# RWKV-7 outputs as rows of head and token, a unit's own products in one run, Gram products that alternate between heads, and value rows centred ahead

## The chip, the core and the metric

The kernel runs on one core of one Trainium2 chip. The core has five engines that work side by side: TensorE (PE in the profile; PEld is its weight load), VectorE (DVE), ScalarE (ACT), GpSimd (POOL) and SyncE (SP), whose queue issues nearly all DMAs here. PE writes PSUM alone: 128 partitions with eight banks of 512 float32 each. The metric is the device time of one execution in microseconds (us); the median over several runs is compared.

## The reference

One attention layer and one recurrent layer over 1024 latent and 256 context tokens, 1024 features. The change lies in the recurrent layer's RWKV-7 branch (512 features, 8 heads of 64), which runs over the tokens in both directions, the context first:

```python
def step(s, inp):                      # s: 64x64 per head
    r_t, w_t, k_t, v_t, kk_t, b_t = inp
    sa = jnp.einsum('bhij,bhj->bhi', s, kk_t)
    s = s * w_t[:, :, None, :] - sa[..., None] * b_t[:, :, None, :] + v_t[..., None] * k_t[:, :, None, :]
    y = jnp.einsum('bhij,bhj->bhi', s, r_t) if emit else None
    return s, y
...
yf = y.astype(jnp.float32)             # y: both directions' sum
mean = jnp.mean(yf, axis=-1, keepdims=True)
var = jnp.mean(jnp.square(yf - mean), axis=-1, keepdims=True)
yn = ((yf - mean) * lax.rsqrt(var + RWKV_GN_EPS)).reshape(y.shape[:2] + (BRANCH_W,))
yn = (yn * gn_w + gn_b).astype(v.dtype)
bonus = jnp.sum(r * k_bonus * r_k, axis=-1, keepdims=True) * v
```

Each row i of the state takes in its own value `v_t[i]` alone, so an output's 64 values depend linearly on the 64 values of `v`; `mean` and `var` go over these 64.

## The kernel before

All is float32; a float32 product shows as two records on PE, a transpose as one. Layer 1 first projects its inputs and, per head pair `j` (128 features), stores to DRAM the keys and normalised keys (`KK`, by `rw_keys`), the values as rows of tokens (`VT`, by `rw_values`: ten PE transposes for each of four pairs), the receptance (`US`), decays (`SG`) and rates (`AS`).

The recurrence is worked in chunks of 64 tokens. A **unit** is four chunks (256 tokens, block `q`; `q == 0` is the context and gives no output) of one head pair `j` in one direction `d`: 8 jobs of 5 units, 40 units, 32 of them latent. A unit goes through these functions:

- `rw_front` loads its inputs, makes running sums of the decays (`cs_ps`), takes their exponentials into `E`, `AK`, `AR`, scales them by the keys and the receptance (L1505, L1506), forms `BK`, and multiplies per head and chunk `BK` by `AKR` (the Gram products, `g_ps`, L1533: 64 rows of the array, 128 columns; head 0 rows 0 to 63, head 1 rows 64 to 127). The result is masked into `la` (DVE) and `gm` (ACT copy, POOL mask). Transposes of `BK` give `BT`; `AK` and the products `la` by `V` fill `R` (`rh_ps`).
- `rw_invert` inverts a job's 32x32 blocks in 31 steps of two DVE instructions (L1586, L1588), spread over other work by `PACE`.
- `rw_solve` makes `At` and `UV` from `R` in three products; `rw_trans` makes `PH` (carries the state over a chunk) and `RT` (what the state adds to a chunk's outputs).
- `rw_scan` goes chunk by chunk: `BT` by `UV` and `PH` by the last state `S` add up in `st_ps`; ACT scales that into the next `S` (L1674). Two ACT copies put `S` into a 128x128 block-diagonal tile `sd` (L1681); `RT` by `sd` and, per head, `gm` by `UV` add up in `yo_ps`, with tokens as rows and both heads' features as columns. `Y` takes the sum, then adds the other direction's.
- `rw_bonus` and `rw_readout` close a block once both directions are done: mean (L1721, L1722), centring (L1724), variance, scale, two transposes (`yt_ps`), gate, store.

Block-wise order in `rwkv`: for unit `b`, `upto("s", b + 2)`, `fronts(b + 12)`, `upto("t", b + 1)`, bonus, scan, and from `b >= 28` `Final.after(b)`, the output projection (`fe_ps`). The first ten fronts run ahead, five between projections of layer 1. This order is only what is traced: a planner that simulates the engines puts each engine's instructions in order, bound by data, by buffers and by explicit edges. `tc.keep_in_program_order(ins)` is such an edge: `ins` comes behind the instruction traced just before it on its engine, but others may come in between. `rw_invert` has raised priority.

PSUM banks in this stage: tag `f` two (all five tiles of a front after the tenth: `cs_ps`, two `g_ps`, `bk_ps`, `rh_ps`; later `fe_ps`), `s` one, `p` two, `t`, `y`, `r` one each; `PB` and `FB` are these counts.

Of the kernel before, what the change touches and what calls it, by code (L numbers as in the profile page):

```python
# [29 lines left out]
def constants():  # L30
# [5 lines left out]
    c["k_ones2"] = b  # L36
    p = np.zeros((128, 128), np.float32)
# [37 lines left out]
    gm[0, :, 0], gm[0, :, 1] = tc_ > sr, tc_ >= sr  # L75
    gm[1, :, 0], gm[1, :, 1] = tc_ < sr, tc_ <= sr
# [44 lines left out]
PB = (1, 1, 1, 1, 1)  # L121
# [52 lines left out]
class K:  # L174
# [1064 lines left out]
    def rw_init(self):  # L1239
# [12 lines left out]
        tri = fp.tile([128, 2, 256], F32, name="tri0", tag="kkf", bufs=2)  # L1252
        nc.sync.dma_start(out=tri, in_=a["k_tri"].rearrange("d p k -> p d k"))
        C["tri"] = fp.tile([128, 2, 256], F32R, name="tri", bufs=1)
        nc.vector.tensor_copy(out=C["tri"], in_=tri)
# [34 lines left out]
    def rw_pre(self, sp):  # L1290
        nc, a = self.nc, self.a
        self.ones2 = sp.tile([128, 128], F32, name="ones2k")
        nc.sync.dma_start(out=self.ones2, in_=a["k_ones2"])
        self.e12 = sp.tile([128, 1], F32, name="e12")
        nc.vector.memset(self.e12, 1e-12)
# [74 lines left out]
    def rwkv(self):  # L1370
        nc, tc, a = self.nc, self.tc, self.a
        with ExitStack() as st:
# [13 lines left out]
            C["S"] = [kp.tile([128, 128], F32, name=f"S{i}") for i in range(4)]  # L1386
            self.ns = 0
# [5 lines left out]
            def fronts(n):  # L1393
                while self.nf < min(n, 40):
                    invert(PACE[0])
                    self.rw_next_front()
                    if self.nf == 10:
                        for t in C["S"]:
                            nc.vector.memset(t, 0.0)

            def upto(what, n):
                while done[what] < min(n, 40):
# [20 lines left out]
            for b in range(40):  # L1423
# [8 lines left out]
                if i == 0 and d == 0:  # L1432
                    Y = wp.tile([128, 8, 128], F32, name="Y", bufs=2)
# [28 lines left out]
    def rw_front(self, F, q, wp, bufs):  # L1462
# [5 lines left out]
        tags = [(t, dict(zip("sptyrf", PB + (FB,)))[t]) for t in ("sfff" if self.nfront < 5 else "rfty" if self.nfront < 10 else "ffff")]  # L1468
# [23 lines left out]
        AK, AR = AKR[:, :, 0, :], AKR[:, :, 1, :]  # L1492
        nc.scalar.activation(out=AK, in_=ps[:, :, 128:256], func=AF.Exp, scale=K0)
# [6 lines left out]
        kv, kf = v3(kk[:, 0]), v3(kk[:, 1])  # L1500
# [23 lines left out]
        W = 128 if lat else 64  # L1524
        for h in range(2):
            z = slice(64 * h, 64 * h + 64)
            ps = self.rps([128, 4, 128], "g_ps", *tags[1])
            for ci in range(4):
                i, c = divmod(ci, 2)
                zc = slice(64 * c, 64 * c + 64)  # L1530
                w = BK[z, i, 128 * c:128 * c + 128]
                x = AKR[z, i, :, zc] if lat else AK[z, i, zc]
                nc.tensor.matmul(ps[:, ci, 0:W], w, x, start=True, stop=True)  # L1533
            nc.vector.tensor_tensor(out=la[:, h], in0=ps[:, :, 0:64], in1=mask[:, 0:64].unsqueeze(1).to_broadcast([128, 4, 64]),
                                    op=ALU.mult)
            if lat:
                nc.scalar.copy(out=gm[:, h], in_=ps[:, :, 64:128])
# [619 lines left out]
```

## Time and profile before

| | |
|---|---|
| median of 3 runs | 2480.39 us (2474.9 to 2482.06) |
| profiled execution | 2487.22 us |
| its span | 2485.4 us, 45290 instructions |
| PE, PEld busy | 2275.4 us, 1892.6 us |
| DVE, ACT, POOL busy | 1568.8 us, 1177.3 us, 931.4 us |
| HBM | 145 GB/s over the span |

The span runs from the first to the last profiled instruction; 1.8 us of the profiled execution lie around it. Matmuls are pipelined and a record's end is modelled, so that a record's time holds a tail in which the next one already runs; start-to-start distances say what a record costs its successor. The granted clock is that of PE: 1.0 is 2.4 GHz, 0.5 is 1.2 GHz.

### The profile page before, as it was taken

The page shows a single profiled execution, that of the slowest core. Times are in us where ns is not written, and L with a number is a line of the kernel's source. Part 1 is how long each engine was busy: PE and PEld are TensorE (multiplying, and loading weights), DVE is VectorE, ACT ScalarE, POOL GpSimd, SP SyncE. Part 2 cuts the span into 40 slices and gives each one's busy share as a digit, 9 for nine tenths or more (in the row PEclk, how much of TensorE's full clock was granted, in tenths as well). Part 3 has the DMA queues.
Part 4 walks back from the last instruction along what each step waited for, and adds up shares of the span by engine and source line. Part 5 has one row for each costly group of instructions (what it writes and reads, how often), then busy time and mean ns, then how long its engine had stood idle before and what let it go on. Part 6 is the DMA issues. An engine that isn't in the chain of part 4 may idle for free. (4 is left out here: it accounts for less than half of the span.)

```text
span 2485.4 us, 45290 instructions
## 1 busy us (share of the span) xinstructions
PE 2275.4 (92%) x16647; PEld 1892.6 (76%) x16647; DVE 1568.8 (63%) x3175; ACT 1177.3 (47%) x2695; POOL 931.4 (37%) x959
## 2 busy tenths in 40 slices
PE   4999999999999989779899889999968999998997
PEld 3877888777878877668778778788757877887775
DVE  6255532368667867455486696457797776777425
ACT  5354434456556555532323221366435656665334
POOL 1253235201011654511033244224745464655512
PEclk8999999999999989889999999999858989999999
DMA  8433344682222766843454544574534343444522
GB/s 280 132 123 119 126 147 146 196 254 93 80 68 90 200 199 183 225 165 110 144 164 150 164 158 136 173 257 134 155 85 131 107 122 97 115 134 126 168 73 92
DMA packets 351428, 361.69 MB, mean 146 GB/s; under 512 B 83106, under 2 KB 283055, under 8 KB 350438
## 3 DMA queue, kind: packets, MB, share of 16 engines
q1 hardware_dynamic: 341894, 330.34, 43.5%
q10 hardware_dynamic: 9168, 24.25, 3.2%
q0 software_dynamic: 144, 4.19, 0.4%
q8 instruction: 132, 2.16, 0.4%
q14 instruction: 90, 0.74, 0.1%
HBM read 260.07 MB, written 100.10 MB: 145 GB/s over the span
## 5 line engine op out<-in xcount | busy, mean ns | idle before, releaser
L158 PE MATMUL g_ps<-xl,w_hi 128*128 128x512 f32 x1056 | 268.0, 399 | 1.0 <-ACT w_hi L192 1.0
L158 PEld LDWEIGHTS g_ps<-xl,w_hi 128*128 128x128 f32 x1056 | 198.9, 191 | 44.0 <-issue 1.9
L158 PE MATMUL s_ps<-k,q 128*128 128x256 f32 (+1 forms) x704 | 199.9, 381 | 7.6 <-DVE pn L700 4.3
L441 POOL TENSOR_TENSOR al_acc<-al_acc,al_t 128x512 f32<-128x512 f32 x98 | 129.0, 1316 | 185.6 <-ACT al_t L439 155.5
L196 DVE TENSOR_TENSOR w_lo<-w_raw,w_hi 128x256 fp32r<-128x256 f32 (+1 forms) x184 | 131.2, 769 | 86.6 <-PE g_ps L158 45.3
L187 ACT COPY pt<-pt_ps 128x512 f32<-128x512 f32 (+1 forms) x203 | 102.1, 506 | 139.3 <-PE pt_ps L161 133.7
L1586 DVE TENSOR_TENSOR tmp<-L,X 80x112 f32<-80x112 f32 (+25 forms) x279 | 136.4, 489 | 17.8 <-DMA L<-LD 8.9
L1588 DVE TENSOR_TENSOR X<-X,tmp 80x112 f32<-80x112 f32 (+25 forms) x279 | 140.6, 504 | 6.5
L158 PE MATMUL g_ps<-xl,w_lo 128*128 128x512 f32 x528 | 137.8, 395 | 0.0
L161 PE MATMUL pt_ps<-ident,p 128*128 128x128 f32 x704 | 118.1, 283 | 17.7 <-DVE pt L185 7.5
L158 PE MATMUL g_ps<-xhi,w_hi 128*128 128x512 f32 (+1 forms) x528 | 118.2, 366 | 8.9 <-DVE ac_res L283 4.7
L161 PEld LDWEIGHTS pt_ps<-ident,p 128*128 128x128 f32 x704 | 80.8, 141 | 52.9 <-DVE pt L185 14.8
L158 PEld LDWEIGHTS s_ps<-k,q 128*128 128x128 f32 x704 | 109.9, 200 | 14.6 <-DVE p L700 7.1
L695 ACT ACTIVATE p<-p,mn 128x1280 f32<-128x1280 f32 (+1 forms) x96 | 103.4, 1077 | 35.7 <-DVE p L700 35.5
L439 ACT ACTIVATE al_t<-al_w,condT 128x512 f32<-128x512 f32 x98 | 70.8, 722 | 101.7 <-POOL al_acc L441 60.9
L158 PE MATMUL g_ps<-xhi,w_lo 128*128 128x512 f32 (+1 forms) x528 | 118.2, 362 | 0.0
L881 POOL TENSOR_TENSOR bias<-namask,tt 128x384 f32<-128x384 f32 x64 | 67.5, 1055 | 125.9 <-DVE mn L890 52.0
L158 PEld LDWEIGHTS g_ps<-xl,w_lo 128*128 128x128 f32 x528 | 98.2, 188 | 21.1 <-issue 1.4
L158 PE MATMUL g_ps<-xlo,w_hi 128*128 128x512 f32 (+1 forms) x528 | 112.8, 356 | 0.0
L158 PEld LDWEIGHTS g_ps<-xhi,w_hi 128*128 128x128 f32 x528 | 90.0, 194 | 29.5 <-DVE qraw L549 5.4
L158 PE MATMUL g_ps<-AKR,BK 64*128 64x128 f32 (+1 forms) x640 | 91.1, 335 | 22.6 <-DVE AKR L1505 14.8
L158 PEld LDWEIGHTS g_ps<-xhi,w_lo 128*128 128x128 f32 x528 | 89.0, 189 | 18.9 <-issue 5.8
(438 smaller groups left out, 5869.4 us busy)
## 6 DMA issues: line engine op xcount, KB each, us to landing
w_raw<-rec_w_in SPq DMA_DIRECT2D x33, 512.0 KB
hfw<-FW SPq DMA_DIRECT2D x32, 512.0 KB
w_raw<-attn_w_in SPq DMA_DIRECT2D x13, 1024.0 KB
al_w<-rec_ada_w SPq DMA_DIRECT2D x48, 256.0 KB
tt<-TG SPq DMA_DIRECT2D x64, 192.0 KB
kkf<-KK SPq DMA_DIRECT2D x40, 256.0 KB
q<-qb SPq DMA_DIRECT2D x64, 128.0 KB
HS<-hs SPq DMA_DIRECT2D x32, 256.0 KB
```

The costliest lines, as they stand in the source:

```text
L158: return self.keep(self.pe.matmul(*args, **kw))
L161: return self.keep(self.pe.transpose(*args, **kw))
L187: self.nc.scalar.copy(out=out, in_=in_)
L196: e.tensor_tensor(out=lo, in0=full, in1=hi.bitcast(F32), op=ALU.subtract)
L439: nc.scalar.activation(out=o, in_=wt, func=AF.Copy, scale=self.condT[:, k, ci:ci + 1])
L441: nc.gpsimd.tensor_tensor(out=t, in0=t, in1=o, op=ALU.add)
L695: self.nc.scalar.activation(out=p, in_=p, func=AF.Exp, bias=mn, scale=-1.0, accum_out=rs)
L881: nc.gpsimd.tensor_tensor(out=b, in0=mask, in1=tt, op=ALU.subtract)
L1586: nc.vector.tensor_tensor(out=tv, in0=L[:, s:s + 1, rt].to_broadcast([n, nj, nt]), in1=X[:, rj, s:s + 1].to_broadcast([n, nj, nt]), op=ALU ...
L1588: nc.vector.tensor_tensor(out=X[:, rj, rt], in0=X[:, rj, rt], in1=tv, op=ALU.subtract)
```

## The change

- `rw_values` multiplies by `k_cent` (identity less 1/64 within each head) where it transposed by the identity, so that the stored value rows have no mean over a head's 64 features. `rw_readout` drops the mean and its subtraction. The bonus still takes the values as they were, from `US`.
- In `rw_front` the receptance is loaded into the first third of a larger `kkf` (two buffers; the tile `rf` with three goes), right behind the `KK` load. `AR` and `AK` swap places in `AKR`, and for latent units one Exp and one product of 512 columns replace two of 256 each. The masks swap to match.
- The Gram products of both heads are written into two `g_ps` tiles in turn: chunk 0 of head 0, of head 1, chunk 1 of head 0, and so on, each behind the one before by an edge.
- A new `rw_own`, called after `rw_trans`, forms a unit's products with its own vectors (`BT` by `UV`, `gm` by `UV`, alternating between heads) in one run of 16, into one bank `sy_ps` of tag `y`: part 0 for the states, part 1 for the outputs, with 64 rows for each head. Tag `y` gets two banks, tag `t` goes.
- `rw_scan` adds `PH` by `S` and `RT` by `S` to it, per head as 64x64 products in opposite quarters of the array. The block-diagonal tiles and their copies go. Outputs are rows of (head, token) and 64 columns; `Y` is 16 x 64 per row, and `rw_readout` turns it back with eight products by 64x64 identities where it had two transposes.

```diff
+    c["k_cent"] = (np.eye(128) - b / 64).astype(np.float32)
...
-    gm[0, :, 0], gm[0, :, 1] = tc_ > sr, tc_ >= sr
-    gm[1, :, 0], gm[1, :, 1] = tc_ < sr, tc_ <= sr
+    gm[0, :, 0], gm[0, :, 1] = tc_ >= sr, tc_ > sr
+    gm[1, :, 0], gm[1, :, 1] = tc_ <= sr, tc_ < sr
...
-PB = (1, 1, 1, 1, 1)
+PB = (1, 1, 2, 1)
...
-                nc.tensor.transpose(ps[:, q, :], o[:, (t4 + q) * 128:(t4 + q + 1) * 128], self.ident)
+                nc.tensor.matmul(ps[:, q, :], o[:, (t4 + q) * 128:(t4 + q + 1) * 128], self.cent, start=True, stop=True)
...
                         self.rw_trans(fr[k], q)
+                        self.rw_own(fr[k], q)
...
-                    Y = wp.tile([128, 8, 128], F32, name="Y", bufs=2)
+                    Y = wp.tile([128, 16, 64], F32, name="Y", bufs=2)
...
-        kk = fp.tile([128, 2, 256], F32, name="kkf", bufs=2)
-        nc.sync.dma_start(out=kk, in_=self.KK[rows, q])
+
+        kk = fp.tile([128, 3, 256], F32, name="kkf", bufs=2)
+        nc.sync.dma_start(out=kk[:, 1:3], in_=self.KK[rows, q])
+        if lat:
+            nc.sync.dma_start(out=kk[:, 0], in_=self.US[rows, q * 256:q * 256 + 256])
...
-        AK, AR = AKR[:, :, 0, :], AKR[:, :, 1, :]
-        nc.scalar.activation(out=AK, in_=ps[:, :, 128:256], func=AF.Exp, scale=K0)
+        AR, AK = AKR[:, :, 0, :], AKR[:, :, 1, :]
+        if lat:
+            nc.scalar.activation(out=AKR, in_=ps.rearrange("p i (a t) -> p i a t", a=2), func=AF.Exp, scale=K0)
+        else:
+            nc.scalar.activation(out=AK, in_=ps[:, :, 128:256], func=AF.Exp, scale=K0)
...
         if lat:
-            nc.scalar.activation(out=AR, in_=ps[:, :, 0:128], func=AF.Exp, scale=K0)
-            rf = fp.tile([128, 256], F32, name="rf", bufs=3)
-            nc.sync.dma_start(out=rf, in_=self.US[rows, tok])
-            nc.vector.tensor_tensor(out=AR, in0=AR, in1=v3(rf), op=ALU.mult)
-        nc.vector.tensor_tensor(out=AK, in0=AK, in1=kv, op=ALU.mult)
+            nc.vector.tensor_tensor(out=AKR, in0=AKR, in1=kk[:, 0:2].rearrange("p a (i t) -> p i a t", t=128), op=ALU.mult)
+        else:
+            nc.vector.tensor_tensor(out=AK, in0=AK, in1=kv, op=ALU.mult)
...
-        W = 128 if lat else 64
+        c0 = 0 if lat else 64
+        gp = [self.rps([128, 4, 128], "g_ps", *tags[1 + h]) for h in range(2)]
+        for ci in range(4):
+            i, c = divmod(ci, 2)
+            zc = slice(64 * c, 64 * c + 64)
+            for h in range(2):
+                z = slice(64 * h, 64 * h + 64)
+                ins = nc.tensor.matmul(gp[h][:, ci, c0:128], BK[z, i, 128 * c:128 * c + 128],
+                                       AKR[z, i, :, zc] if lat else AK[z, i, zc], start=True, stop=True)
+                if ci or h:
+                    self.tc.keep_in_program_order(ins)
         for h in range(2):
-            z = slice(64 * h, 64 * h + 64)
-            ps = self.rps([128, 4, 128], "g_ps", *tags[1])
-            for ci in range(4):
-                i, c = divmod(ci, 2)
-                zc = slice(64 * c, 64 * c + 64)
-                w = BK[z, i, 128 * c:128 * c + 128]
-                x = AKR[z, i, :, zc] if lat else AK[z, i, zc]
-                nc.tensor.matmul(ps[:, ci, 0:W], w, x, start=True, stop=True)
-            nc.vector.tensor_tensor(out=la[:, h], in0=ps[:, :, 0:64], in1=mask[:, 0:64].unsqueeze(1).to_broadcast([128, 4, 64]),
+            ps = gp[h]
+            nc.vector.tensor_tensor(out=la[:, h], in0=ps[:, :, 64:128], in1=mask[:, 64:128].unsqueeze(1).to_broadcast([128, 4, 64]),
                                     op=ALU.mult)
             if lat:
-                nc.scalar.copy(out=gm[:, h], in_=ps[:, :, 64:128])
+                nc.scalar.copy(out=gm[:, h], in_=ps[:, :, 0:64])
                 nc.gpsimd.tensor_tensor(out=gm[:, h], in0=gm[:, h],
-                                        in1=mask[:, 64:128].unsqueeze(1).to_broadcast([128, 4, 64]), op=ALU.mult)
+                                        in1=mask[:, 0:64].unsqueeze(1).to_broadcast([128, 4, 64]), op=ALU.mult)
...
+    def rw_own(self, F, q):
+
+        nc = self.nc
+        G = F["g"][q]
+        gm, UV, BT = (G[n] for n in ("gm", "UV", "BT"))
+        sy = G["sy"] = self.rps([128, 2, 4, 64], "sy_ps", "y", PB[2])
+        for ci in range(4):
+            i, c = divmod(ci, 2)
+            for part in range(2 if q > 0 else 1):
+                for h in range(2):
+                    zo = slice(64 * h, 64 * h + 64)
+                    ins = nc.tensor.matmul(sy[zo, part, ci, :], gm[:, h, ci, :] if part else BT[:, ci, zo], UV[:, i, c, h, :],
+                                           start=(ci == 0 and part == 0), stop=False, skip_group_check=True,
+                                           tile_position=(0, 64 * h))
+
+                    if ci or part or h:
+                        self.tc.keep_in_program_order(ins)
+
     def rw_scan(self, F, q, Y):
 
         nc, wp = self.nc, self.wp
         d, Dt = F["d"], F["Dt"]
         G = F["g"].pop(q)
-        gm, UV, PH, BT = (G[n] for n in ("gm", "UV", "PH", "BT"))
+        sy, PH, RT = G["sy"], G["PH"], G["RT"]
         lat = q > 0
         n0 = 4 * q + (2 if d == 0 else 0)
         heads = [(h, slice(64 * h, 64 * h + 64)) for h in range(2)]
-        yp = self.rps([128, 2, 128], "yo_ps", "y", PB[3])
-        RT = G["RT"] if lat else None
         for ci in (range(4) if d == 0 else range(3, -1, -1)):
             i, c = divmod(ci, 2)
             S = F["S"]
-            ps = self.rps([128, 64], "st_ps", "t", PB[2])
-            n = wp.tile([128, 64], F32, name="S", bufs=4)
-            for h, zo in heads:
-                nc.tensor.matmul(ps[zo], BT[:, ci, zo], UV[:, i, c, h, :], start=True, stop=(S is None), tile_position=(0, 64 * h))
             if S is not None:
                 for h, zo in heads:
-                    nc.tensor.matmul(ps[zo], PH[zo, i, c, :], S[zo], start=False, stop=True, tile_position=(64 * h, 64 * h))
-            nc.scalar.activation(out=n, in_=ps, func=AF.Copy, scale=Dt[:, n0 + ci:n0 + ci + 1])
-            F["S"] = n
+                    nc.tensor.matmul(sy[zo, 0, ci, :], PH[zo, i, c, :], S[zo], start=False, stop=True, skip_group_check=True,
+                                     tile_position=(64 * h, 64 * h))
+            n = F["S"] = wp.tile([128, 64], F32, name="S", bufs=4)
+            nc.scalar.activation(out=n, in_=sy[:, 0, ci, :], func=AF.Copy, scale=Dt[:, n0 + ci:n0 + ci + 1])
             if lat:
-                zc = slice(64 * c, 64 * c + 64)
-                self.ns = (self.ns + 1) % 4
-                sd = self.C["S"][self.ns]
                 for h, zo in heads:
-                    nc.scalar.copy(out=sd[zo, zo], in_=S[zo])
-                nc.tensor.matmul(yp[zc, i, :], RT[:, i, c, :], sd, start=True, stop=False, tile_position=(0, 64 * c))
-                for h, zo in heads:
-                    nc.tensor.matmul(yp[zc, i, zo], gm[:, h, ci, :], UV[:, i, c, h, :], start=False, stop=(h == 1),
-                                     tile_position=(0, 64 * c))
+                    nc.tensor.matmul(sy[zo, 1, ci, :], RT[zo, i, c, :], S[zo], start=False, stop=True, skip_group_check=True,
+                                     tile_position=(64 * h, 64 * h))
         if lat:
-            yv = Y[:, 2 * q - 2:2 * q, :]
+            yv = Y[:, 4 * q - 4:4 * q, :]
             if d == 0:
-                nc.scalar.copy(out=yv, in_=yp)
+                nc.scalar.copy(out=yv, in_=sy[:, 1])
             else:
-                nc.vector.tensor_tensor(out=yv, in0=yv, in1=yp, op=ALU.add)
+                nc.vector.tensor_tensor(out=yv, in0=yv, in1=sy[:, 1], op=ALU.add)
 
...
-        Yq = Y[:, 2 * q - 2:2 * q, :]
-        y = Yq.rearrange("p a (h f) -> p (a h) f", h=2)
-        mu = wp.tile([128, 4], F32, name="gmu")
-        nc.vector.tensor_reduce(out=mu, in_=y, axis=AX.X, op=ALU.add)
-        nc.vector.tensor_scalar(out=mu, in0=mu, scalar1=-1.0 / 64, scalar2=None, op0=ALU.mult)
+
+        y = Y[:, 4 * q - 4:4 * q, :]
         b16 = lambda t: t.unsqueeze(2).to_broadcast([128, 4, 64])
-        nc.vector.tensor_tensor(out=y, in0=y, in1=b16(mu), op=ALU.add)
...
-        ps = self.rps([128, 2, 128], "yt_ps", "r", PB[4])
-        for i in range(2):
-            nc.tensor.transpose(ps[:, i, :], Yq[:, i, :], self.ident)
+        ps = self.rps([128, 4, 64], "yt_ps", "r", PB[3])
+        for ci in range(4):
+            for h in range(2):
+                zo = slice(64 * h, 64 * h + 64)
+                nc.tensor.matmul(ps[zo, ci, :], y[zo, ci, :], self.ident[zo, zo], start=True, stop=True,
+                                 tile_position=(64 * h, 64 * h))
```

Left out: the load of `k_cent`, the removal of the `S` tiles and their memsets, the tags of early fronts (`"rfty"` becomes `"rfyy"`, so that fronts 6 to 10 put the second head into tag `y`), and renumbered entries of `PB`.

## Rows read from the trace of the kernel before

**Rows 1.** The page, part 1: busy time, share of the span, instructions.

```profile
PE 2275.4 (92%) x16647; PEld 1892.6 (76%) x16647; DVE 1568.8 (63%) x3175; ACT 1177.3 (47%) x2695; POOL 931.4 (37%) x959
```

**Rows 2.** Windows: stretch, length, busy us by engine, granted clock, DMA share, GB/s.

```profile
1600.00:1800.00 200.00, 192.25 (x1005) 158.54 (x1004) 137.28 (x174) 118.63 (x240) 90.65 (x91) 0.96 0.55 178
1815.00:1865.00 50.00, 30.81 (x187) 24.89 (x186) 47.21 (x104) 16.28 (x47) 21.78 (x28) 0.50 0.33 86
1890.00:2400.00 510.00, 489.13 (x5131) 404.30 (x5129) 347.03 (x773) 292.49 (x952) 270.43 (x366) 0.93 0.43 121
```

**Rows 3.** Waits, 1890 to 2400 us: us in total, times, longest.

```profile
PE w_ps L158 <- DVE R L1620: 5.4, 2, 3.7
PE g_ps L158 <- DVE AKR L1505: 5.3, 3, 3.8
```

**Rows 4.** The chain that ended last, 1890 to 2400 us: shares, then pieces.

```profile
by line: PE yo_ps L158 10.2%; PE fe_ps L158 10.1%; PE st_ps L158 9.8%; PE g_ps L158 7.4%; PE y_ps L158 5.9%; PE w_ps L158 5.8%; PE z_ps L158 5.7%; issue 4.8%; PE ph_ps L158 4.2%; DVE X L1588 4.0%; DVE tmp L1586 4.0%; PE rh_ps L158 2.1%; PE 
...
1980.60 7.35 issue
...
2207.57 2.55 DMA rf<-US
```

**Rows 5.** Timeline, scan chunks on PE: start us, us busy, engine, line, operation.

```profile
1901.15 0.43 PE L158 MATMUL yo_ps<-S,RT 128*64 128x128 f32 x2
...
1902.12 0.43 PE L158 MATMUL yo_ps<-S,RT 128*64 128x128 f32 x2
...
1915.01 0.34 PE L158 MATMUL st_ps<-UV,BT 128*64 128x64 f32 x4
...
1915.28 0.33 PE L158 MATMUL st_ps<-S,PH 64*64 64x64 f32 x4
...
1915.54 0.43 PE L158 MATMUL yo_ps<-S,RT 128*64 128x128 f32 x2
...
1915.81 0.40 PE L158 MATMUL yo_ps<-UV,gm 128*64 128x64 f32 x4
...
1916.13 0.94 PE L158 MATMUL y_ps<-R,XT 128*128 128x128 f32 x6
```

**Rows 6.** Timeline: products in alternating row halves, then a full one.

```profile
1905.75 0.68 PE L158 MATMUL rh_ps<-V,la 64*64 64x64 f32 x16
...
1906.36 1.16 PE L158 MATMUL z_ps<-Z,LO 128*128 128x128 f32 x8
```

**Rows 7.** The chain, pieces of 1788 to 1800 us and one later: Gram products.

```profile
1788.56 3.02 PE g_ps L158 x16
...
1795.28 2.00 PE g_ps L158 x8
...
1897.97 1.64 PE g_ps L158 x16
```

**Rows 8.** One tile's instructions (`AKR`), 1890 to 2400 us: ns least, median, most; starts.

```profile
L158 PE MATMUL g_ps<-AKR,BK x432: 272/272/579, 1897.9 to 2258.9; 64*128 64x128 f32 x118, 64*128 64x64 f32 x26
```

**Rows 9.** Groups by line and form on PE: busy us, mean ns, idle before.

```profile
L161 PE MATMUL yt_ps<-ident,Y 128*128 128x128 f32 x32 | 7.6, 319 | 1.3 <-DVE Y L1739 1.3
L161 PE MATMUL vt_ps<-ident,rwo 128*128 128x128 f32 x40 | 7.0, 273 | 0.7 <-DVE rwo L1119 0.7
```

**Rows 10.** Groups by line on ACT and DVE, from 1750 us on.

```profile
L1681 ACT COPY S<-S 64x64 f32<-64x64 f32 x256 | 62.1, 243 | 4.2
L1674 ACT ACTIVATE S<-st_ps,Dt 128x64 f32<-128x64 f32 x160 | 50.5, 316 | 82.2 <-PE st_ps L158 80.1
...
L1502 ACT ACTIVATE AKR<-cs_ps 128x256 f32<-128x256 f32 x32 | 12.9, 404 | 0.0
...
L1724 DVE TENSOR_TENSOR Y<-Y,gmu 128x256 f32<-128x256 f32 x16 | 7.6, 478 | 0.3
...
L1721 DVE TENSOR_REDUCE gmu<-Y 128x4 f32<-128x256 f32 x16 | 6.6, 412 | 0.2
...
L1722 DVE TENSOR_SCALAR gmu<-gmu 128x4 f32<-128x4 f32 x16 | 5.6, 350 | 0.2
```

More of the change, by code (lines that the diff above doesn't have):

```diff
@@ L1251, in rw_init @@
         C = self.C = {}
-        tri = fp.tile([128, 2, 256], F32, name="tri0", tag="kkf", bufs=2)
-        nc.sync.dma_start(out=tri, in_=a["k_tri"].rearrange("d p k -> p d k"))
+        tri = fp.tile([128, 3, 256], F32, name="tri0", tag="kkf", bufs=2)
+        nc.sync.dma_start(out=tri[:, 0:2], in_=a["k_tri"].rearrange("d p k -> p d k"))
         C["tri"] = fp.tile([128, 2, 256], F32R, name="tri", bufs=1)
-        nc.vector.tensor_copy(out=C["tri"], in_=tri)
+        nc.vector.tensor_copy(out=C["tri"], in_=tri[:, 0:2])
         C["gm"] = fp.tile([128, 2, 128], F32, name="gm", bufs=1)
@@ L1293, in rw_pre @@
         nc.sync.dma_start(out=self.ones2, in_=a["k_ones2"])
+        self.cent = sp.tile([128, 128], F32, name="cent")
+        nc.sync.dma_start(out=self.cent, in_=a["k_cent"])
         self.e12 = sp.tile([128, 1], F32, name="e12")
@@ L1385, in rwkv @@
             C["LO"].append([kp.tile([128, 4, 128], F32, name=f"LO1{i}") for i in range(5)])
-            C["S"] = [kp.tile([128, 128], F32, name=f"S{i}") for i in range(4)]
-            self.ns = 0
             jobs, seq, fr = self.jobs, self.seq, self.fr
@@ L1396, in fronts @@
                     self.rw_next_front()
-                    if self.nf == 10:
-                        for t in C["S"]:
-                            nc.vector.memset(t, 0.0)
             def upto(what, n):
@@ L1467, in rw_front @@
         self.nfront = getattr(self, "nfront", -1) + 1
-        tags = [(t, dict(zip("sptyrf", PB + (FB,)))[t]) for t in ("sfff" if self.nfront < 5 else "rfty" if self.nfront < 10 else "ffff")]
+        tags = [(t, dict(zip("spyrf", PB + (FB,)))[t]) for t in ("sfff" if self.nfront < 5 else "rfyy" if self.nfront < 10 else "ffff")]
         rows = slice(j * 128, j * 128 + 128)
         K0 = math.exp(-0.5)
-        kk = fp.tile([128, 2, 256], F32, name="kkf", bufs=2)
-        nc.sync.dma_start(out=kk, in_=self.KK[rows, q])
+        kk = fp.tile([128, 3, 256], F32, name="kkf", bufs=2)
+        nc.sync.dma_start(out=kk[:, 1:3], in_=self.KK[rows, q])
+        if lat:
+            nc.sync.dma_start(out=kk[:, 0], in_=self.US[rows, q * 256:q * 256 + 256])
         af = fp.tile([128, 256], F32, name="af", bufs=3)
@@ L1709, in rw_bonus @@
         nc.vector.scalar_tensor_tensor(out=a0, in0=a0, scalar=self.col("rwkv_r_k", j), in1=r, op0=ALU.mult, op1=ALU.mult)
-        ps = self.rps([128, 256], "bo_ps", "r", PB[4])
+        ps = self.rps([128, 256], "bo_ps", "r", PB[3])
         nc.tensor.matmul(ps, C["ones2"], a0, start=True, stop=True)
@@ L1739, in rw_readout @@
         nc.vector.tensor_tensor(out=y, in0=y, in1=b16(vr), op=ALU.mult)
-        ps = self.rps([128, 2, 128], "yt_ps", "r", PB[4])
-        for i in range(2):
-            nc.tensor.transpose(ps[:, i, :], Yq[:, i, :], self.ident)
+        ps = self.rps([128, 4, 64], "yt_ps", "r", PB[3])
[4 more added lines that the diff above has]
+                                 tile_position=(64 * h, 64 * h))
         t = wp.tile([128, 256], F32, name="yo", tag="ro", bufs=2)
-        nc.scalar.activation(out=t, in_=ps.rearrange("p i f -> p (i f)"), func=AF.Identity,
+        nc.scalar.activation(out=t, in_=ps.rearrange("p i t -> p (i t)"), func=AF.Identity,
                              scale=self.col("rwkv_gn_w", j), bias=self.col("rwkv_gn_b", j))
```

2 lines of the change are left out of this document (1 added, 1 removed).

## The prediction

> **What bounds the kernel now.** I read the page's head first: TensorE (PE) is busy 92% of the span and no other engine passes 63%, so the first question is whether PE's busy time is real [rows 1]. The view by windows puts the change in its place. The recurrence of the RWKV heads fills the stretch from 1890 to 2400 us; there PE is busy 489 of 510 us at a mean granted clock of 0.93, VectorE (DVE) 347, ScalarE (ACT) 292, GpSimd (POOL) 270. Just ahead of it, from 1815 to 1865 us, DVE is busy 47 of 50 us and PE 31: that is the first block inversion, and PE work saved there is worth nothing [rows 2]. A mean of 0.93 between the levels 1.0 and 0.5 means some 14% of the stretch, 71 us, at 1.2 GHz.
>
> The waits of PE in that stretch are few: the two longest entries are 5.4 and 5.3 us in total [rows 3]. So PE is not starved; its queue is full of small products. But the chain that ended last is not PE alone. Its account for 1890 to 2400 us lists nine PE names with 10.2+10.1+9.8+7.4+5.9+5.8+5.7+4.2+2.1 = 61%, and DVE's two inversion lines with 8% (the tail of the list is cut off) [rows 4]. I therefore let 65% of what PE saves there reach the end; the rest falls where DVE, POOL or a transfer sets the pace and PE would only wait sooner.
>
> **The scan.** A unit is 256 tokens of one head pair in one direction: 32 latent units and 8 context ones. Per chunk of 64 tokens the kernel issues four groups of records (an f32 matmul leaves two): own state product (UV,BT, 4 records), state carry (S,PH, 4), carried output (S,RT, 2 of 128 columns), own output (UV,gm, 4). One such chunk alone takes, start to start, 0.27 + 0.26 + 0.27 + 0.32 = 1.12 us; one that follows another takes 0.97 [rows 5]. I take 1.05, or 4.2 us per latent unit.
>
> What the new forms cost is read from a neighbour: 16 records of V,la, 64x64 and alternating between the array's two row halves, run from 1905.75 to the next product at 1906.36, 0.61 us; 4 records show 0.33 us busy and 16 show 0.68, so a further record adds 0.35/12 = 0.029 us [rows 5, 6]. Where both heads use the same columns, as UV,gm does now, 4 records take 0.40 [rows 5], so records do overlap when neighbours use different parts of the array. The new run of a unit's own products alternates between heads: 32 records, 0.61 + 16 x 0.029 = 1.08 us. A chunk then has the carry and the carried output, both 64x64 and both needing only the previous state: 8 records back to back 0.26 + 4 x 0.029 = 0.38 us, or 0.52 if something comes between them. A latent unit becomes 1.08 + 4 x 0.38 = 2.6 us, or 3.2 in pieces. The saving is 1.6 or 1.0 us; since the edges that keep the run in order allow other products in between, I take 1.3, times 32 = 42 us. A context unit goes from 4 x 0.53 = 2.1 to 0.61 + 4 x 0.26 = 1.65 us: 8 x 0.45 = 4 us. Together 46 us, between 36 and 55.
>
> Carry, carried output and the readout's new products write one bank from both row halves of the array. So does V,la now, 16 records in 0.61 us [rows 6], which is why I let the halves overlap. A rule of the Trainium skill speaks against it: "TensorEngine Tiling (Array Packing)", Restrictions and Gotchas, says that different row tiles cannot access the same PSUM bank at the same time. By that rule the sum below would hold 21 us of PE instead of 57, as the third rival works out; by the row it stands.
>
> **Gram products.** Now eight records of one head follow eight of the other, 64 rows of the array each: 1.64 us at full clock, 3.02 at half, while one head's eight take 2.00 at half [rows 7]. So the heads already overlap at the seam. Alternating, 16 records should cost what 8 of one head do: 2.00/3.02 = 0.66 of the run, a saving of 0.55 us at full clock and 1.02 at half. 27 of the 40 fronts lie from 1897.9 us on [rows 8]: 27 x 0.55 / 0.93 = 16 us. Of the 13 earlier ones about five count, the others lie under the inversion: 4 us. Together 20, between 12 and 25. Both banks must be free at the start; the second one's last reader is ACT's Exp of the same front, which the product waits for anyway, so I cost that at nothing.
>
> **What PE gains in work.** The readout turns two transposes into eight f32 products, 16 records: 0.61 us against 7.6/16 = 0.48 busy with its tail, some 0.3 us more on the queue without that tail, 16 x 0.3 = 5 us [rows 6, 9]. Centring in `rw_values` makes 40 transpose records into 80 product records; they cost what 128-column products cost, 1.16 us busy for 8 with a tail of 0.27, so 0.11 each: 4.5 us [rows 6, 9]. The latter lie between 1600 and 1800 us, where PE is busy 192 of 200 us [rows 2], and count in full.
>
> **The other engines.** ACT loses 256 block copies, 62.1 us, and one start in each of 32 Exp (I take 0.2 of 0.404 us, 6 us); DVE loses the mean of the readout, 6.6 + 5.6 + 7.6 = 19.8 us, and one start in each of 32 products (I take 0.15 of the 0.478 us that such a one takes, 5 us) [rows 10]. ACT is no listed part of the chain, so its 68 us count nothing; for DVE's 25 I take an eighth, 3 us, by its listed share of 8% and something for the cut tail [rows 4].
>
> **Costed at nothing.** The masks only change places; the zeroed state blocks go; the constant for centring is one 64 KB load long before use. The receptance load moves into `kkf`: it has two buffers instead of three, and on SP it goes ahead of `af`, `sg`, `V`, with the block inverses and the solver's values queued behind. It waits for the same release that the `kkf` load beside it already waits for. If that cover is gone, a front waits as for the one such load in the chain, 2.55 us [rows 4]; ten such waits would be 25 us, the lower bound for this edit.
>
> **Sum.** PE: -46 - 20 + 5 = -61 in the stage, of which 65% arrive, -40; +4.5 ahead of it; DVE -3: -38.5 us. I round to -40 for a shorter step from state to state (two block copies of 0.243 us no longer stand between ACT's state and the carried output [rows 10]). From the profiled execution's 2487.2 us that gives 2447; the median of the runs is 6.8 us below it, so 2440. Bounds: 55 + 25 - 9.5 = 71 us of PE all arriving and 5 of DVE give 2404; 36 + 12 - 12 = 36 us with half arriving give 2462.
>
> **Rivals.**
> Everything arrives (2404): PE's short waits [rows 3] speak for it, the chain's DVE stretches [rows 4] against. Chance 0.15.
> The clock takes it back (2475): the granted clock is 0.50 where PE is busy 31 of 50 us and 0.93 where it is busy 489 of 510 [rows 2]. If the unrealised third of the saving becomes idle time and the half-clock share doubles from 71 us, 71/2 = 35 us of the 40 are lost. Against: PE stays above 85% busy. The Trainium skill's "TensorE: Matmul & The Clock Gate", Part 1, tells the same tale, the clock being released by activity and dropped in idleness; the trace agrees, 0.50 against 0.93. Chance 0.12.
> The row halves take turns (2463): if the two records of a pair followed each other at 2 x 0.029 = 0.058 us, four pairs make a chunk 0.23 us longer, 128 x 0.23 = 29 us, and eight pairs a readout 0.46, 16 x 0.46 = 7 us; of 57 us of PE 21 are left, 65% of them 14, and 3 of DVE. Against it stand the 0.61 us [rows 6]. This is what the array-packing page of the Trainium skill would make of the new products. Chance 0.05.
> Slower, the state's step becomes the bound (2500): state and outputs now share one bank, so ACT's read of a state (0.316 us [rows 10]) and the next outputs' products exclude each other; if outputs go first, each step gets 0.26 us longer, 128 x 0.26 = 33 us, and PE's saving turns into waiting: from 2480, 20 to 33 us slower with what DVE gives back. It decides only when four steps of a unit fill its share of the stretch, 510/36 = 14 us; now a step can be 0.97 us apart [rows 5]. Chance 0.08; a new order with fresh stalls of the kind at 1980.60 (7.35 us [rows 4]) several times over is the 0.03 beside it.
> The forecast (2425 to 2462) keeps 0.57.
>
> **Numbers.** A difference of 0.3% (7.4 us) is about what a measurement of this kernel can tell from none. Faster: 0.57 + 0.15 + 0.05 and a third of the clock's case, 0.81; same 0.08; slower 0.11. The range leaves out the slower cases and a little beyond full arrival: 2400 to 2484, the likeliest case alone 2404 to 2462.
>
> **What would show it.** Right: the groups for S,RT with 64 columns near 0.03 us a record beside S,PH; 16 alternating Gram records near 1.1 us at full clock; no ACT block copies; PE's busy time in the stage down by about 60 us and the stage some 35 to 40 us shorter; PE waits grown. Wrong: 64-column pairs 0.058 us apart (row halves), a lower mean clock with the same busy time (clock), or `PE <- ACT S` waits of several hundred nanoseconds at each step (state).

## The result and the profile after

The changed kernel takes 2459.99 us (median of 4 runs, 2455.95 to 2463.09) against 2477.64 of the kernel before in the same runs: a ratio of 0.9926, 95% interval 0.9902 to 0.9951. It is 18 us faster; 40 were forecast. The direction held and the time lies in the range, but the gain is much smaller than forecast.

Part 1 of the page after, to be read against [rows 1]:

```profile
PE 2212.4 (90%) x17167; PEld 1839.0 (75%) x17167; DVE 1548.4 (63%) x3091; ACT 1103.4 (45%) x2403; POOL 927.3 (38%) x959
```

PE lost 63 us of busy time, ACT 74, DVE 20. So the work went away, but the time did not fall by as much. Where it stayed is seen when both kernels are cut at the same events: the last `i_ps` product of the projections, the second unit's first state (ACT's `S`), and the last state. Windows of the kernel before at these events (stretch, length, busy time by engine, granted clock, DMA share, GB/s):

```profile
1565.00:1896.00 331.00, 292.45 (x1652) 242.41 (x1651) 227.63 (x376) 162.17 (x364) 146.00 (x158) 0.85 0.50 159
1896.00:2455.00 559.00, 538.46 (x5497) 442.27 (x5496) 367.45 (x828) 315.14 (x1028) 280.24 (x387) 0.94 0.42 118
```

The same windows of the changed kernel:

```profile
1570.00:1888.00 318.00, 277.98 (x1674) 230.32 (x1674) 214.99 (x327) 151.08 (x338) 141.99 (x150) 0.89 0.51 160
1888.00:2431.00 543.00, 485.62 (x5977) 397.32 (x5978) 359.95 (x796) 253.01 (x762) 278.38 (x394) 0.93 0.45 125
```

From the first state on (called the stage below) PE is busy 538.5 - 485.6 = 53 us less, and the stage is only 16 us shorter: PE's idle time grew from 20.5 to 57.4 us. Ahead of the stage 14.5 us of PE and 13 us of time went, but at a clock of 0.89 instead of 0.85: some 70 us of 318 at 1.2 GHz instead of 99 of 331. Sixteen Gram records took 3.02 us at half the clock and 1.64 at full [rows 7], so a microsecond at half the clock costs at most about 0.46 us (an estimate from these two). The 29 us could thus be worth 13 us by themselves, and what went ahead of the stage is not shown to come from the change. Up to the last projection the two programs do almost the same, and the two profiles still differ by 5 us (in all kernels below this point lies between 1563 and 1574 us): differences of a few microseconds between single profiles mean nothing.

The waits of PE in the changed kernel's stage (1888 to 2431 us; total, times, longest), beside [rows 3]:

```profile
PE w_ps L160 <- DVE R L1629: 14.0, 9, 4.0
PE bk_ps L163 <- ACT gm L1546: 11.8, 11, 1.6
PE sy_ps L160 <- ACT S L1697: 6.5, 9, 1.7
```

And the head of its chain for the same stretch, below that of the kernel before between the same events (1896 to 2455 us; [rows 4] has 1890 to 2400):

```profile
by line: PE fe_ps L158 14.4%; PE yo_ps L158 10.5%; PE st_ps L158 10.2%; PE g_ps L158 6.8%; PE y_ps L158 5.7%; PE z_ps L158 5.5%; PE w_ps L158 5.5%; PE ph_ps L158 4.3%; issue 4.2%; DVE tmp L1586 3.6%; DVE X L1588 3.5%; PE rh_ps L158 1.9%; PE
...
by line: PE fe_ps L160 13.4%; PE sy_ps L160 8.4%; DVE tmp L1595 7.4%; issue 6.7%; DVE X L1597 6.3%; PE y_ps L160 3.9%; PE w_ps L160 3.3%; PE ph_ps L160 2.7%; DMA L<-LD 2.6%; PE z_ps L160 2.5%; PE g_ps L160 2.3%; DMA LD<-la 1.7%; DMA iob<-AS
```

Both lists are cut off at their end. The listed PE names, 65% of the chain before, are 37% now; the inversion's two DVE lines went from 7 to 14%, and the transfers that carry its blocks (`LD<-la`, `L<-LD`) are listed.

The new forms themselves, on the changed kernel's timeline (start us, us busy, engine, line, operation): a chunk with its next product, a unit's own products, a Gram run with its next product.

```profile
1981.63 0.33 PE L160 MATMUL sy_ps<-S,RT 64*64 64x64 f32 x4
1981.80 0.28 PE L160 MATMUL sy_ps<-S,PH 64*64 64x64 f32 x4
1982.01 0.38 PE L160 MATMUL y_ps<-R,XT 128*128 128x128 f32 x1
...
1986.69 0.34 PE L160 MATMUL sy_ps<-UV,BT 128*64 128x64 f32 x4
...
1987.56 0.29 PE L160 MATMUL sy_ps<-UV,gm 128*64 128x64 f32 x4
1987.77 0.48 PE L160 MATMUL bo_ps<-ioa,ones 128*128 128x256 f32 x1
...
2009.43 1.16 PE L160 MATMUL g_ps<-AKR,BK 64*128 64x128 f32 x16 [0.19 <-POOL BK L1523]
2010.53 0.38 PE L160 MATMUL z_ps<-Z,LO 128*128 128x128 f32 x1
```

Start to start, carry and carried output take 0.38 us, the 32 own records 1.08, the 16 Gram records 1.10. The run of own products is one unit's; in most units other products come between them.

### The profile page after: what moved, and what is told of

The parts are those of the page before. It is cut to its first block, busy times and chain, and to the rows that moved or that the text cites. A ratio compares the mean times of both kernels' runs of the same rounds, so it can differ in the third digit from the quotient of the medians.

```text
span 2461.3 us, 45979 instructions
## 1 busy us (share of the span) xinstructions
PE 2212.4 (90%) x17167; PEld 1839.0 (75%) x17167; DVE 1548.4 (63%) x3091; ACT 1103.4 (45%) x2403; POOL 927.3 (38%) x959
## 5 line engine op out<-in xcount | busy, mean ns | idle before, releaser
L1595 DVE TENSOR_TENSOR tmp<-L,X 80x112 f32<-80x112 f32 (+28 forms) x279 | 136.9, 491 | 25.4 <-DMA L<-LD 17.0
L1597 DVE TENSOR_TENSOR X<-X,tmp 80x112 f32<-80x112 f32 (+28 forms) x279 | 136.1, 488 | 6.6
L160 PEld LDWEIGHTS s_ps<-k,q 128*128 128x128 f32 x704 | 108.9, 198 | 14.5 <-DVE p L702 7.3
L160 PEld LDWEIGHTS g_ps<-xlo,w_hi 128*128 128x128 f32 x528 | 89.6, 191 | 15.8 <-issue 1.9
```

Of the source, the lines that this page charges most:

```text
L160: return self.keep(self.pe.matmul(*args, **kw))
L1595: nc.vector.tensor_tensor(out=tv, in0=L[:, s:s + 1, rt].to_broadcast([n, nj, nt]), in1=X[:, rj, s:s + 1].to_broadcast([n, nj, nt]), op=ALU ...
L1597: nc.vector.tensor_tensor(out=X[:, rj, rt], in0=X[:, rj, rt], in1=tv, op=ALU.subtract)
```

## The experiments

What the kernels below did in the stage is read from one row of the view by windows each, cut at the same two events. Idle is length less PE's busy time.

| kernel | stage us | PE busy | PE idle | clock | median us | ratio to before |
|---|---|---|---|---|---|---|
| before | 559 | 538.5 | 20.5 | 0.94 | 2477.64 | |
| after | 543 | 485.6 | 57.4 | 0.93 | 2459.99 | 0.9926 (0.9902 to 0.9951) |
| e1_gram_only | 547 | 514.2 | 32.8 | 0.97 | 2463.11 | 0.993 (0.9912 to 0.9949) |
| e2_gram_by_head | 540 | 499.4 | 40.6 | 0.93 | 2475.5 | 0.9986 (0.9966 to 1.0005) |
| e12_own_twice | 580 | 531.4 | 48.6 | 0.94 | 2494.99 | 1.0055 (1.0028 to 1.0083) |
| e8_after_gram_twice | 567 | 509.6 | 57.4 | 0.93 | 2503.39 | 1.0086 (1.0057 to 1.0115) |
| e9_before_gram_twice | 602 | 584.1 | 17.9 | 0.96 | 2547.18 | 1.0258 (1.0218 to 1.0298) |
| e3_bk_own_bank | 538 | 487.3 | 50.7 | 0.94 | 2455.67 | 0.9893 (0.9871 to 0.9914) |
| e14_inv_low | 534 | 487.3 | 46.7 | 0.94 | 2456.27 | 0.989 (0.9868 to 0.9913) |
| e16_own_bank_low | 537 | 487.6 | 49.4 | 0.95 | 2467.85 | 0.9928 (0.9907 to 0.9948) |
| e17_before_inv_low | 559 | 532.5 | 26.5 | 0.96 | 2472.39 | 0.9945 (0.9925 to 0.9965) |
| e6_after_loads_on_act | 538 | 483.4 | 54.6 | 0.94 | 2467.19 | 0.9932 (0.9905 to 0.9958) |
| e10_bk_rh_in_r | 543 | 489.4 | 53.6 | 0.92 | 2469.66 | 0.9967 (0.9951 to 0.9984) |
| e18_solve_ahead | 562 | 497.8 | 64.2 | 0.90 | 2477.03 | 0.9969 (0.9951 to 0.9988) |
| e19_trans_ahead | 547 | 468.7 | 78.3 | 0.90 | 2468.9 | 0.9944 (0.9919 to 0.9969) |
| e11_bk_rh_in_two_r | 549 | 468.9 | 80.1 | 0.92 | 2477.57 | 0.999 (0.997 to 1.001) |
| e7_before_loads_on_act | 553 | 523.9 | 29.1 | 0.98 | 2485.47 | 1.0013 (0.9984 to 1.0043) |
| e13_before_bk_rh_in_r | 556 | 533.7 | 22.3 | 0.96 | 2471.04 | 0.9972 (0.9948 to 0.9996) |
| e4_after_half_inv | 524 | 476.9 | 47.1 | 0.93 | 2421.45 | 0.9756 (0.9736 to 0.9777) |
| e5_before_half_inv | 545 | 529.9 | 15.1 | 0.98 | 2442.19 | 0.9828 (0.9794 to 0.9862) |

Three cautions go with these rows. Each stage is one profile: the kernel before and e7, e13 and e17, which leave its scan as it was, need 553 to 559 us in the stage, and 315 to 331 us between the last projection and it. The clock goes with the layout of the scan: 0.94 to 0.98 in the kernels with the old scan (before, e1, e5, e7, e9, e13, e17), 0.90 to 0.95 in those with the new one; and busy time holds the clock. Nor is busy time a fixed cost of the products: e18 and e19 issue the products of the changed kernel, both at a clock of 0.90, and are busy for 497.8 and 468.7 us.

**The parts alone.** e1_gram_only is the kernel before with the Gram loop of the change. e2_gram_by_head is the changed kernel with the old order:

```
-        gp = [self.rps([128, 4, 128], "g_ps", *tags[1 + h]) for h in range(2)]
-        for ci in range(4):
-            ...
-            for h in range(2):
-                ins = nc.tensor.matmul(gp[h][:, ci, c0:128], ...)
+        for h in range(2):
+            ps = self.rps([128, 4, 128], "g_ps", *tags[1])
+            for ci in range(4):
+                nc.tensor.matmul(ps[:, ci, c0:128], ...)
```

> The kernel before with one part of the change, the Gram products alternating between heads. Theory W (the alternation brings a new wait: both banks fill at once, so the transposes of BK wait for ACT's copy of the first head's block, which waits for DVE's mask): PE saves 0.55 us a front but waits some 0.5 us a front more at bk_ps, and the time stays within 5 us of before (ratio 0.998 to 1.002). Theory D (no particular wait; what PE saves arrives as far as PE sets the pace, two thirds in the kernel before): 16 to 20 us of PE saved, 10 to 13 us arrive, ratio 0.995 to 0.996.

> The changed kernel with the Gram products head by head again, without the edges that keep them in order. W: the wait of bk_ps for ACT's gm copy falls from 13 us back to below 3 us and the loss of 0.55 us a front is made good by it: as fast as the changed kernel or up to 5 us faster (2455 to 2460 us; 0.990 to 0.993 of before). D: PE is not what paces the changed kernel, so 20 us more PE work cost 5 to 10 us (2465 to 2470 us; 0.995 to 0.997).

The alternation alone brings 17.6 us in its runs (2480.72 to 2463.11), as much as the whole change. The rest alone is within measurement of nothing, although it takes 39 us of PE's time out of the stage. The window of e2, below that of e1, shows half of that turned into waiting: 540 us, 40.6 of them idle. The other half, a stage 19 us shorter, is in this profile; of the medians, 5 us apart, it is not clear.

```profile
1885.00:2432.00 547.00, 514.23 (x5565) 418.53 (x5566) 373.44 (x851) 320.89 (x1049) 283.51 (x387) 0.97 0.43 120
...
1906.00:2446.00 540.00, 499.43 (x5947) 410.52 (x5942) 343.17 (x767) 249.37 (x755) 281.19 (x390) 0.93 0.45 124
```

The stage of e1 is 12 us shorter with 24 us less of PE, but at a clock of 0.97: some 33 us at 1.2 GHz where the kernel before had 67, which could be worth 16 us by the estimate above. Going on from e2 to the changed kernel, both at 0.93, alternation takes another 14 us of PE's time in the stage and none of its length. So no profile shows that the alternation makes the stage shorter; the profiles differ ahead of it, where e2 needs 334 us and the changed kernel 318 (331 before, 314 in e1), at clocks of 0.85 and 0.89 (0.85 and 0.86). Both theories missed: e1 gained more than either allowed, and e2 is slower than either said.

**More work on PE.** If PE no longer sets the pace, added work must vanish in the new idle time. e8 and e9 issue the Gram products twice, in the changed kernel (`for rep in range(2):` around the loop) and in the one before (`for ci in (0, 1, 2, 3) * 2:`); e12 does so with the changed kernel's own products, which are on no front's chain.

> The changed kernel with each front's alternating Gram products done twice into the same place: 0.9 us of PE more for each of 40 fronts at full clock, 36 us, results unchanged. If PE's time still reached the end by two thirds: 20 to 25 us slower than the changed kernel (1.000 to 1.003 of before). Q and L: PE has 43 us of waits to fill up to unit 27, a third or less arrives, 5 to 12 us (0.9945 to 0.9975).

> The kernel before with each head's Gram products done twice: 1.3 us of PE more for each of 40 fronts, some 50 us, results unchanged. PE waits for 12 us up to unit 27 only, so at least two thirds arrive: 30 to 45 us slower than before (1.012 to 1.018). Were the pace set elsewhere in this kernel too, 15 us or less (below 1.006).

> The changed kernel with each unit's own products done twice into the same place, 32 records or 1.0 us more of PE for 32 latent units and half for 8, some 36 us, all of it off the fronts' chain; results unchanged. F: PE has waits to fill, a third or less arrives, 0 to 12 us slower than the changed kernel (0.993 to 0.997 of before), where the same 36 us put into the Gram products cost 40. If PE's time as such sets the pace: 25 to 40 us slower (1.003 to 1.009).

It does not vanish. In e12 PE is busy 45.8 us more in the stage and the stage grows by 37 us; in e8 both grow by 24; in e9 45.6 us of PE and 43 of time. The window of e12:

```profile
1887.00:2467.00 580.00, 531.39 (x7100) 436.37 (x7100) 363.17 (x793) 254.48 (x762) 283.94 (x395) 0.94 0.43 116
```

In medians e8 is 43 us over the changed kernel, e12 35, and e9 65 over the kernel before: e8 and e9 cost more than any theory allowed. Work that is added arrives by 80 to 100% in the stage, work that was taken away by 30%, or by half in e2. The idle time is not slack that more work fills. One doubt stays: e12's products stand between a unit's solve and its scan, so that part of their price can be that of this chain.

**One wait at a time.** e3 sends the transposes of b and k to the bank of tag r after the tenth front. The second head's Gram products have the same entry of `tags` and move with them, so it tests both together. e14 gives the inversion's steps the ordinary priority, e16 does both, e17 does the second to the kernel before.

```
-... else "rfyy" if self.nfront < 10 else "ffff")]
+... else "rfyy" if self.nfront < 10 else "ffrf")]

-            with self.tc.high_priority(1000):
-                if next(self.inv[0], 1):
+            if next(self.inv[0], 1):
```

> The changed kernel with bk_ps of the fronts after the tenth in the bank of tag r instead of f. The transposes of BK then wait for no Gram block. W: the 13 us that PE waits at bk_ps go and 8 to 13 us arrive: 2447 to 2452 us, 0.988 to 0.989 of before. D: PE only waits elsewhere, as for DVE's R: 0 to 4 us arrive, 2456 to 2460 us, 0.991 to 0.993.

> The changed kernel with the inversion's steps at the ordinary priority instead of 1000. Theory Q2, the largest new wait (the product w behind VectorE's subtraction R, 14.0 us in the stage) is there because steps of the inversion stand ahead of R in VectorE's queue: the wait falls to a few us and the time by 8 to 15 us, to about 2445 to 2452. Theory P, the waits follow from the whole order that the planner writes, and one wait removed comes back at another place: the wait on R falls, others rise, the time stays within 6 us of 2460. Against both: the inversions come late for the solve, and the wait on the loads of the inverses grows; the time then rises over 2470.

> The changed kernel with the transposes of b and k, and the second head's Gram products, in the bank of tag r after the tenth front (2455.67 us by itself), and with the inversion's steps at the ordinary priority. Theory Q2: the two waits are different ones, and what each edit brings adds up: 2440 to 2448. Theory P: 2452 to 2460, no better than the one edit alone.

> The kernel before with the inversion's steps at the ordinary priority: the same edit without the change. Theory Q2: before the change the wait on R is 5.4 us, so the edit brings 5 us or less, 2473 to 2478. Theory P: within 6 us of 2478. If the inversions come late, over 2485.

Each edit alone lies 4 us under the changed kernel in the median, which is not clear of noise: their intervals (0.9871 to 0.9914, 0.9868 to 0.9913) overlap with that of the changed kernel. Together they take 2467.85 us, 12 us over either, where the theory of separate waits that add up said 2440 to 2448: it is refuted. Theory P's 2452 to 2460 was missed by 8 us too, and in the profile the stage of e16 (537 us) is as short as theirs. e17 gives the kernel before 10 us by the priority alone (0.9945), more than theory Q2 allowed where the wait on `R` was 5.4 us; so what e14 gains need not come from the new wait. PE's waits in the stage of e3:

```profile
PE w_ps L160 <- DVE R L1629: 15.8, 11, 4.6
...
PE bk_ps L163 <- ACT gm L1546: 0.8, 3, 0.4
```

Of e14:

```profile
PE bk_ps L163 <- ACT gm L1545: 11.0, 13, 1.7
PE g_ps L160 <- DVE AKR L1509: 8.0, 8, 1.7
PE w_ps L160 <- DVE R L1628: 5.0, 4, 1.9
```

And of e16:

```profile
PE w_ps L160 <- DVE R L1628: 12.8, 11, 3.3
PE g_ps L160 <- DVE AKR L1509: 6.4, 5, 2.7
```

The bank takes away the wait on `gm` (11.8 to 0.8 us) and leaves that on `R` at 15.8. The wait on `R` falls from 14.0 to 5.0 us by the priority and is back at 12.8 once the transposes have their bank; the wait on `gm` stays in the one and is no longer among the longest in the other. What remains is the sum: 50.7, 46.7 and 49.4 us idle.

**Other suspects.** e6 issues the loads of the bonus and of V on ACT's queue instead of SP's (the new `kkf` load stands ahead of others on SP). e10 gives the transposes and the `rh_ps` products the bank of tag r, so that the fronts' two banks carry less. e18 issues each solve a unit earlier (`upto("s", b + 3)`), e19 the transition matrices and own products (`upto("t", b + 2)`).

> The changed kernel with the six loads of each block's bonus and the two V loads of each front issued from ACT's queue instead of SP's, 176 issues of some 0.5 us off SP. Theory Q (SP's queue, 252 of 342 us busy with issuing between the second state and unit 27 of the changed kernel, is what paces it now that PE needs less): 10 to 20 us faster than the changed kernel, 2440 to 2450 us (0.984 to 0.988 of before). Theory L (no one queue paces it; PE waits on many short steps of in-order queues): within 4 us of the changed kernel (0.991 to 0.994).

> The changed kernel with bk_ps and rh_ps of the fronts after the tenth in the one bank of tag r, so that only cs_ps and the two g_ps take turns in the two banks of f. Theory F (the fronts run one behind the other through the two banks of f, and one front's own chain, 12.6 us from its first cs_ps record to ACT's copy into R, sets the 13.2 us from front to front): the next cs_ps can start when the Gram blocks are read, some 4 us earlier; PE fills its waits and 10 to 25 us are gained on the changed kernel, 2435 to 2450 us (0.982 to 0.988 of before). If PE's own time or many short waits set the pace: within 4 us of the changed kernel (0.991 to 0.994).

> The changed kernel with each unit's solve issued one unit earlier (three units ahead of the scan instead of two). Theory K, TensorE waits (57 us of its time between the second unit's first state and the last state) because in the new layout too little other work stands between a product and the one that needs its result, in the solve first of all (the product w behind VectorE's R, 14 us): with a unit's more distance the wait on R falls under 5 us, TensorE's idle time to some 40 us and the time by 10 to 15 us, to 2445 to 2450. Theory P, the waits follow from the whole order that the planner writes and come back at another place: idle time 45 to 60 us, time 2452 to 2466.

> The changed kernel with each unit's transition matrices and own vectors' products issued one unit earlier (two units ahead of the scan instead of one). Theory K: what the scan's products wait for is done a unit earlier, the order has more work to put between, idle time of TensorE under 45 us and the time 2445 to 2452. Theory P: idle time 45 to 60 us, time 2452 to 2466. Against both: the own products fill both banks of the scan a unit early, the scan waits for a bank, and the time rises over 2470.

None shortens the time; idle time is 54 to 78 us there. e6 agrees with theory L by its ratio; e10, e18 and e19 are 10, 17 and 9 us slower than the changed kernel, outside every range that the theories gave. The queue of loads, the fronts' banks and the distance between a unit's steps are thereby out as single causes, as far as an edit that also changes the planner's order can tell. Three more are in the table: the loads on ACT's queue do nothing for the kernel before (e7), two banks for r with one for the scan bring the changed kernel back to the time of before (e11), and the two tiles in r bring the kernel before some 7 us (e13).

**DVE's inversion.** e4 and e5 leave out every second step of the inversion, in the changed kernel and in the one before.

```
-        for s in (range(31) if d == 0 else range(31, 0, -1)):
+        for s in (range(0, 31, 2) if d == 0 else range(31, 0, -2)):
```

> The changed kernel with every second step of the block inversions left out (16 or 15 of 31 steps are done, the results are not the inverses): some 135 us of DVE time less, PE, ACT and transfers unchanged. D: DVE's queue is what PE now waits for; PE's idle time in the stage falls from 59 to 30 us or less and, with the first inversion some 20 us shorter before the stage, 45 to 60 us arrive: 2400 to 2415 us (0.969 to 0.975 of before). W: only the inversion ahead of the stage gets shorter and the bk_ps waits stay: 2430 to 2440 us (0.981 to 0.985).

> The kernel before with every second step of the inversion on VectorE left out (the output is then not the reference's): the pair of the same cut in the changed kernel, which gave 2421.45 us, some 38 us below the changed kernel's 2460. Theory N, VectorE became the next bound only because the change freed TensorE: before the change TensorE waits 20 us in the stage, so the cut has little to take there, and the time falls by 15 us or less, to about 2463 to 2477. Theory A, VectorE's inversion is paid for alike in both kernels (through the clearing of banks and the planner's order, not through the waits that are new): it falls by about as much as in the changed kernel, 35 to 45 us, to about 2435 to 2443.

Both gain about as much, 39 and 41 us, as theory A for the kernel before said; for the changed kernel neither D nor W fits, since idle time falls to 47.1 us and not to 30. But the gains are not in the same place: before the change 32 of it lie ahead of the stage (331 to 299 us, the first inversion) and 14 in it, where PE's busy time falls by 9 at a clock of 0.98 instead of 0.94; after the change 13 lie ahead and 19 in the stage, at the same clock of 0.93. So half of the inversion, some 95 us of DVE, is worth 19 us to the new stage. It is a part of its pace, as the chain's 14% say, and not alone the bound.

## Why the prediction was wrong in size

**What held.** The costs of the new forms, all taken from neighbours [rows 5 to 7], were right where the records follow each other: a chunk 0.38 us, a unit's own products 1.08, both as forecast to the hundredth; Gram 1.10 against 0.66 x 1.64 = 1.08. The readout's and the centring's products cost what was put down, 4.2 us (5 forecast) and 5.3 (4.5), by these groups beside [rows 9] (busy us, mean ns, idle before):

```profile
L160 PE MATMUL vt_ps<-cent,rwo 128*128 128x128 f32 x80 | 12.3, 275 | 0.3 <-DVE rwo L1121 0.3
...
L160 PE MATMUL yt_ps<-ident,Y 64*64 64x64 f32 x256 | 11.8, 224 | 1.4 <-DVE iov L1728 0.8 <-DVE Y L1751 0.4
```

One reading was not: five of the 27 fronts costed at 0.55 us are context fronts, whose products are 64 columns wide, and over all eight of these the Gram products take 15.8 us where they took 16.3. PE's whole busy time fell by 63 us against -61 + 4.5 = -56.5. Part of this agreement is luck, for the parts agree less: 41 us in e1 (20 forecast) and 28 in e2 (36.5), at different clocks. ACT and DVE lost 74 and 20 us where 68 and 25 were forecast; what that was worth was not tested.

**The step that failed** is "65% of what PE saves there reach the end". In the stage 16 of 53 us did, 30%; in e2, without the alternation, 19 of 39, 49%. (The profiled pair is 24 us apart, 16 and 13 less 5 up to the last projection; the medians are 18 apart.) The share was read from the chain of the kernel before [rows 4], which tells which work ended last with PE as slow as it was. It does not tell what ends last once PE is quicker: then PE stands at products that need the subtraction `R`, the copy `gm` or the state `S`, which it used to reach after they were done, most of the time: 29 waits and 32.3 us in the first three rows of its waits, where the kernel before had five on `R` and `S`, 6.9 us. Adding work to PE still costs nearly full price (e12, e8), so a test that only adds would not have shown the step to be wrong. That the time lies within the bounds of the likeliest case is luck: 2462 was made of 36 us of PE with half arriving, and 53 us with 30% come to about as much. Grown waits of PE stood in the prediction as a sign of its being right, and none of its signs of being wrong showed.

**The rivals.** Everything arrives: no. Row halves taking turns: no; eight records of two row halves, all writing one bank, took 0.38 us, where turns would give 0.61. The trace speaks against the rule of the Trainium skill's "TensorEngine Tiling (Array Packing)", Restrictions and Gotchas, that different row tiles cannot access one PSUM bank at the same time, for these f32 products. The state's step: PE waits for ACT's `S` 6.5 us in all, 9 times, no bound. The clock: it does not explain the whole miss, for its mean is 0.943 over the four runs of the changed kernel as over 101 runs of the kernel before, and in the stage of the profiled pair it is 0.93 against 0.94, some 76 us at 1.2 GHz against 67, worth 4 us at most by the estimate above. But the new scan goes with a lower clock in the stage (0.90 to 0.95 against 0.94 to 0.98), and no run tells how much of a stage's length is the clock's. This rival is not out.

**What stays open.** Shown is that the idle time of the stage goes with the new scan layout (40.6 us without the alternation, 47 to 80 in every kernel with both, against 32.8 with the alternation alone and 15 to 29 with neither), that it went with no single wait, bank, queue or priority that was tried, and that work added fills 9 us of it at most (e12). A planner writes the order of all queues beforehand with its own prices, and each of these edits made it write another order; that the waits come from that order is argued, not shown. An order with the chip's measured prices was not tried, nor was the clock's share separated.

The fastest versions, e3 and e14, are 25 and 27 us faster than the kernel before in their own runs (0.9893 and 0.989), not clear of the changed kernel.

## What to carry to other kernels

The share of a saving that arrives cannot be read from the chain alone: an engine that is busy 96% of a stage may be a step ahead of several others at once, and then the price of adding work (here 80 to 100%) says nothing on the worth of removing it (30 to 49%). Cut both profiles at the same events and compare length, busy time and clock; what idle time has grown by is where the gain went, once the clocks agree. When removing one wait brings another at another place, count the sum of waits, not the wait.

## What the runs showed of the hardware

The granted clock and the time go together in unchanged code. Of 101 runs of the kernel before, the 26 with a mean granted clock up to 0.940 have a median of 2486.2 us, the 30 with 0.946 or more 2475.8; a straight line through all gives 1.27 us for each 0.001. If the line holds for other kernels too, which no run here shows, it gives an estimate for the siblings: e2_gram_by_head ran at 0.936 (mean of 12 runs) where before ran at 0.944 beside it, which by this line is 11 us, over half of the 19 us by which its stage was shorter; for e10 (0.936), e18 and e19 (0.937, 0.938) it gives 6 to 10 us. The Trainium skill's "TensorE: Matmul & The Clock Gate", Part 1, lets idleness bring the clock down; the two stages with the lowest clock here, 0.90, have 64 and 78 us of idle time, that of e5 with 0.98 has 15. The order is loose: e7 has 29 us at 0.98, e11 80 at 0.92.
